# Value and decode products with fp32 operands, 64 weight columns at a time, in place of rounded parts

## The chip, the cores and the metric

The kernel runs on one core of one Trainium2 chip. The metric is the device time in microseconds. Three runs of the kernel before took 702.85, 704.45 and 705.08 us; their median is 704.45.

## The reference

One layer of a hybrid encoder for 1024 prompt tokens and 32 sample tokens, width 1024. A combined projection of the normalized input gives q, k, v, a gate, and the input and gate of a state-space branch. The attention is "stick-breaking": no softmax, strictly causal, 8 heads of 64.

```
z = einsum('bqhd,bkhd->bhqk', q, k) / sqrt(64)
mask = k_pos[None, :] < q_pos[:, None]
log_rem = where(mask, log_sigmoid(-z), 0.0)
after = cumsum(log_rem, axis=3, reverse=True) - log_rem
w = where(mask, exp(log_sigmoid(z) + after), 0.0)
att = einsum('bhqk,bkhd->bqhd', w, v)
```

The 32 sample tokens attend to a cache of 1024 keys and values and to themselves. Then each branch is normalized, gated and multiplied by the output weights, and the sum with the input is normalized.

## The kernel before

Its tensors are fp32. A product at fp32 accuracy is made of rounded parts: an operand is rounded to the type fp32r (the "high" part, a ScalarE copy), the rest is taken by a subtraction on VectorE (the "low" part), and two or three matmuls of such parts are summed in PSUM.

The stages, in order of time: input, projections and the state-space branch (to about 265 us); then the attention pipeline, into which the remaining projections and the state-space half of the output product are woven (to about 632 us); then the attention half of the output product.

The pipeline (`pipeline`, from L1439) has 32 units: 4 pairs of heads, 2 heads h, and 4 query groups j of 256 tokens. A unit's first part (`s1_unit`, L1179) makes the scores of two query blocks (L1163), with the mask as a bf16 product (L1165), and ScalarE takes two sigmoids of them into `cb` and `beta`; VectorE runs a product scan over `cb` (L1208), and POOL or VectorE multiplies `beta` by it, which gives the weights. Two units later the second part (`s3_unit`, L1252) transposes the weights on TensorE into a PSUM bank of the tag tr, of which there are two (L1307), and `wt_split` (L1243) makes of the bank the tiles wth (ScalarE) and wtl (VectorE). A visit to the value product (L1270) takes two key blocks: for each, the stacked values vS, 128 columns that hold the high part of 64 channels and the low part, times wth and times wtl, 256 columns. The halves of the sum are added when it is taken out (`end`, L1277). Visits wait in a queue `pvq` that holds at most LAG = 2, or fewer when one of three buffers of wth and wtl is wanted again.

Two decode units stand among the 32 (`DEC`). `decode_s1` (L1332) loads the cache keys into `kc_raw` (two buffers), splits each tile into wth and wtl, and multiplies with a block-diagonal q of 128 columns (BDh, BDl), three matmuls of 512 columns a tile (L1359). `decode_s3` (L1373) transposes the weights, splits them and the cache values, and sums three matmuls of 256 columns a block (L1384).

What stands between these instructions on TensorE is set by `weave` (L1521): each step of the pipeline yields a cost in ns, times a ratio and with corrections by step number (`MORE`), and so much of the projections (L440) or of the output product (L1626) is emitted behind it. Engines run their queues in order; the order is fixed when the program is built.

The form of the changed products is in the kernel before already: L913 multiplies fp32 operands with 64 weight columns, and its four products of a group go to the two halves of the PSUM partitions in turn:

```
for r in range(2):
    for g2 in range(2):
        nc.tensor.matmul(pb[g2 * 64:g2 * 64 + 64, r * NCH:(r + 1) * NCH],
                         WT[:, r, a, g2 * 64:g2 * 64 + 64], U[:, 2 * a + g2],
                         start=True, stop=True)
```

Of the kernel before, what the change touches and what calls it, by code (L numbers as in the profile page):

```python
# [47 lines left out]
LAG = 2  # L48
MORE = {274: 2000, 268: -500, 119: -1000, 144: -500, 150: 1000, 206: -1500, 322: 500, 329: -1000, 17: 2000, 15: -500, 151: 1500, 131: 500, 125: -1500, 209: 1000, 118: -1000, 114: 1000, 112: 500, 190: -1500, 194: 500}
# [18 lines left out]
def hymba_step(ctx, tc, xT, xn, w_in, ln_g, kcT, vc, w_glu, b_glu, w_out, g_att, g_ssm, final_g,  # L68
# [79 lines left out]
    def open_pair0():  # L148
# [11 lines left out]
        vS[0] = p0.tile([128, 8, 256], F32R, name="vS0")  # L160
        for nm in ("BDh", "BDl"):
            Q[nm] = p0.tile([128, 4, 128], F32R, name=nm)
            nc.gpsimd.memset(Q[nm].bitcast(F32), 0.0)
        Q["KSh"] = p0.tile([128, 4, TS], F32R, name="KSh")
        Q["KSl"] = p0.tile([128, 4, TS], F32R, name="KSl")
# [329 lines left out]
    def split_q(p, st):  # L495
        def evac(i, t0, n, ps):
# [8 lines left out]
            if m < n:  # L505
                for hh in range(2):
                    r = slice(64 * hh, 64 * hh + 64)
                    s = 32 * (2 * (p % 2) + hh)
                    act(Q["BDh"][r, p, s:s + 32], qo[r, m:n])
                    tt(Q["BDl"][r, p, s:s + 32], qo[r, m:n], Q["BDh"][r, p, s:s + 32], OP.subtract)  # L510
        return evac

    def split_k(p, st):
        def evac(i, t0, n, ps):
# [11 lines left out]
            if m < n:  # L526
                act(Q["KSh"][:, p], ko[:, m:n])
                tt(Q["KSl"][:, p], ko[:, m:n], Q["KSh"][:, p], OP.subtract)
        return evac

    def split_v(p, st):
        def evac(i, t0, n, ps):
# [3 lines left out]
            def fin():  # L536
# [8 lines left out]
                stack_v(vS[p % 2][:, b0:b0 + nb], pp[:, :nb * 128].rearrange("p (b c) -> p b c", b=nb))  # L545
# [20 lines left out]

    def stack_v(dst, src):

        for hh in range(2):
            act(dst[:, :, 192 * hh:192 * hh + 64], src[:, :, 64 * hh:64 * hh + 64])  # L570
        for hh in range(2):
            tt(dst[:, :, 64 + 64 * hh:128 + 64 * hh], src[:, :, 64 * hh:64 * hh + 64],
               dst[:, :, 192 * hh:192 * hh + 64], OP.subtract)
# [573 lines left out]
    vS[1] = at.tile([128, 8, 256], F32R, name="vS1")  # L1147
# [89 lines left out]
    def w_tiles():  # L1237
        n_w[0] += 1
        while any(i <= n_w[0] - 3 for i, _, _ in pvq):
            pop_pv()  # L1240
        return (at.tile([128, 512], F32R, name="wth", bufs=3), at.tile([128, 512], F32R, name="wtl", bufs=3))

    def wt_split(pp, c0, n, nk=128):  # L1243
        wh, wl = w_tiles()
        if c0:
            for w in (wh, wl):
                nc.gpsimd.memset(w[:, 0:c0].bitcast(F32), 0.0)
        act(wh[:nk, c0:n], pp[:nk, c0:n])
        tt(wl[:nk, c0:n], pp[:nk, c0:n], wh[:nk, c0:n], OP.subtract)
        return wh, wl  # L1250

    def s3_unit(p, h, j, ba, bb_):  # L1252
# [11 lines left out]
        def pv_mm(blocks, wh, wl):  # L1264
            def f():
                if st["n"] == 0:
                    st["ps"] = p_pv()
                for kb, c0 in blocks:
                    for w in (wh, wl):
# [3 lines left out]
                if st["n"] == 2 * nblk:  # L1273
                    end()
            return f
# [19 lines left out]
        for kp in range(j + 1):  # L1295
# [12 lines left out]
            wh, wl = wt_split(pp, 128 if last else 0, 512)  # L1308
            yield 121 * len(lay)
            yield push_pv([n_w[0]], 4 * 262 / 2.4, pv_mm(blocks, wh, wl))  # L1310
# [8 lines left out]
    def k_load(qd, i):  # L1319
        p = 2 * qd + i % 2  # L1320
        kraw[i] = at.tile([128, 512], F32, name="kc_raw", bufs=2)
        nc.sync.dma_start(kraw[i], kcT[p * 128:(p + 1) * 128, 512 * (i // 2):512 * (i // 2) + 512])

    def v_load(qd, i):
        kraw[i] = at.tile([128, 2, 256], F32, name="kc_raw", bufs=2)
# [6 lines left out]
    def decode_s1(qd, out):  # L1332
# [3 lines left out]
        sp = {}  # L1336

        def split(i):
            sp[i] = w_tiles()
            kr = kraw.pop(i)  # L1340
            act(sp[i][0], kr)
            tt(sp[i][1], kr, sp[i][0], OP.subtract)
            if i < 2:
                k_load(qd, i + 2)
            else:
                v_load(qd, i - 2)

        split(0)
        yield 400.0
        for i in range(4):  # L1350
            p = 2 * qd + i % 2
            if i < 3:
                split(i + 1)
            if i % 2 == 0:
                ps = p_z()
            kh, kl = sp.pop(i)
            bh, bl = Q["BDh"][:, p], Q["BDl"][:, p]
            for n, (a, b) in enumerate(((bh, kh), (bl, kh), (bh, kl))):
                nc.tensor.matmul(ps, a, b, start=(i % 2 == 0 and n == 0), stop=(i % 2 == 1 and n == 2))  # L1359
# [5 lines left out]
        mms = []  # L1365
        for p in (2 * qd, 2 * qd + 1):
            bh, bl, kh, kl = Q["BDh"][:, p], Q["BDl"][:, p], Q["KSh"][:, p], Q["KSl"][:, p]
            mms += [(bh, kh, 32), (bl, kh, 32), (bh, kl, 32)]
        z_tile(mms, 32, (c[:, 1024:1056], be[:, 1024:1056]), maskb[:, 128:160])
        yield 7 * 55.0  # L1370
        s1_fin(c, be, CW - 1)

    def decode_s3(qd, be):  # L1373
        st = {"n": 0}

        def mm(blocks, wh, wl, vh, vl, nk, last=False):

            def f():
                if st["n"] == 0:
                    st["ps"] = p_pv()  # L1380
                for i, b in enumerate(blocks):
                    ws = slice(128 * b, 128 * b + 128)
# [532 lines left out]
```

## Time and profile before

| | |
|---|---|
| median of three runs | 704.45 us (702.85 to 705.08) |
| profiled execution | 703.05 us, span 701.2 |
| TensorE matmul busy | 637.0 us, 91%, 3834 instructions |
| TensorE weight loads | 573.0 us, 82% |
| VectorE busy | 503.0 us, 72%, 751 instructions |
| ScalarE busy | 352.3 us, 50%, 805 instructions |
| GpSimd busy | 240.3 us, 34%, 369 instructions |
| granted TensorE clock, mean | 0.952 |

PE is TensorE's matmuls, PEld its weight loads, DVE VectorE, ACT ScalarE, POOL GpSimd. The duration of a matmul holds the time to fill and empty the array; how often one can start is read from the distance of two starts. Line numbers are those of the kernel; operations that go through a helper bear its line (L95 ScalarE, L98 VectorE and GpSimd). A row of the timeline has start, duration, engine, line, operation, out<-in, shape, count, and in brackets the idle time before it with what ended it. A row of the waits has who waited, for whom, us in total, times, the longest. A row of the windows has the stretch and its length, then busy us and instructions running of PE, PEld, DVE, ACT and POOL (those that have any), the granted clock, the DMA share and GB/s.

### The profile page before, as it was taken

What the parts mean: (1) busy time and instruction counts of PE and PEld (TensorE: products, weight loads), DVE (VectorE), ACT (ScalarE), POOL (GpSimd) and SP (SyncE); (2) the same over time, 40 slices, a digit from 0 to 9 for tenths busy, and PEclk for the clock granted to TensorE, in tenths of its full rate; (3) what the DMA queues carried; (4) which work ended last, traced back from release to release, by engine and by line L of the source; (5) the groups of instructions that cost most, each with busy time, mean ns of one, the idle gap of its engine ahead of it and who ended that gap; (6) DMA issues with size and microseconds to landing.
All of it is one profiled execution on the core that took longest, in us unless ns stands there. A gap on an engine that the chain in (4) does not pass through costs nothing. (4 is left out here: it accounts for less than half of the span.)

```text
span 701.2 us, 10842 instructions
## 1 busy us (share of the span) xinstructions
PE 637.0 (91%) x3834; PEld 573.0 (82%) x3834; DVE 503.0 (72%) x751; ACT 352.3 (50%) x805; POOL 240.3 (34%) x369
## 2 busy tenths in 40 slices
PE   7887799989999998999799999989987798989994
PEld 7887689878999997899788898978886586877872
DVE  6987999895254583787787857776768959775653
ACT  6543232431455553567665675465675645642332
POOL 0510110100123377343444424341326513232885
PEclk9987899999999998999999999999999899999998
DMA  8303514822611162101221012222262584518552
GB/s 301 84 31 78 154 31 119 256 75 97 214 56 37 45 241 109 48 31 57 66 77 55 31 62 92 65 74 69 64 208 75 177 267 129 150 68 273 177 177 97
DMA packets 62645, 79.14 MB, mean 113 GB/s; under 512 B 8864, under 2 KB 47072, under 8 KB 62592
## 3 DMA queue, kind: packets, MB, share of 16 engines
q1 hardware_dynamic: 56112, 66.90, 30.1%
q10 hardware_dynamic: 6480, 11.56, 5.3%
q8 instruction: 30, 0.49, 0.3%
q14 instruction: 23, 0.19, 0.1%
HBM read 51.97 MB, written 26.48 MB: 112 GB/s over the span
## 5 line engine op out<-in xcount | busy, mean ns | idle before, releaser
L440 PE MATMUL pj<-xh,w_hi 128*128 128x256 f32 (+2 forms) x456 | 159.4, 350 | 0.0
L440 PE MATMUL pj<-xl,w_hi 128*128 128x256 f32 (+2 forms) x456 | 149.4, 328 | 0.0
L440 PE MATMUL pj<-xh,w_lo 128*128 128x256 f32 (+2 forms) x456 | 149.0, 327 | 0.0
L1208 DVE TENSOR_TENSOR_SCAN cb<-cb 128x896 f32<-128x896 f32 (+8 forms) x66 | 95.9, 1459 | 6.9 <-ACT cb L95 6.2
L440 PEld LDWEIGHTS pj<-xh,w_hi 128*128 128x128 f32 x456 | 88.8, 195 | 4.3 <-issue 2.4
L440 PEld LDWEIGHTS pj<-xl,w_hi 128*128 128x128 f32 x456 | 88.5, 194 | 1.4
L440 PEld LDWEIGHTS pj<-xh,w_lo 128*128 128x128 f32 x456 | 87.9, 193 | 0.3
L95 ACT ACTIVATE cb<-z 128x512 f32<-128x512 f32 (+4 forms) x102 | 49.8, 489 | 50.0 <-PE z L1165 16.5
L98 DVE TENSOR_TENSOR wtl<-tr,wth 128x512 fp32r<-128x512 f32 (+2 forms) x86 | 53.5, 626 | 27.1 <-ACT wth L95 26.0
L1626 PE MATMUL pj<-xh,S 128*128 128x512 f32 (+3 forms) x212 | 69.8, 409 | 0.5 <-ACT w_raw L95 0.5
L98 POOL TENSOR_TENSOR betaL<-betaL,cb 128x896 f32<-128x896 f32 (+2 forms) x24 | 41.7, 1737 | 71.6 <-DVE cb L1208 41.5
L98 POOL TENSOR_TENSOR w_lo<-w_raw,w_hi 128x512 fp32r<-128x512 f32 x30 | 47.0, 1568 | 36.2 <-ACT w_hi L95 36.0
L98 POOL TENSOR_TENSOR betaS<-betaS,cb 128x128 f32<-128x128 f32 (+3 forms) x32 | 27.8, 872 | 72.6 <-DVE cb L1208 54.1
L95 ACT ACTIVATE wth<-tr 128x512 fp32r<-128x512 f32 (+2 forms) x86 | 47.4, 553 | 10.4 <-PE tr L1307 5.9
L1626 PE MATMUL pj<-xl,S 128*128 128x512 f32 (+3 forms) x112 | 43.7, 393 | 0.9 <-DVE xl L98 0.9
L1270 PE MATMUL pv<-wth,vS 128*128 128x256 f32 x160 | 44.2, 297 | 0.1
L1626 PEld LDWEIGHTS pj<-xh,S 128*128 128x128 f32 (+2 forms) x212 | 37.8, 191 | 7.6 <-ACT w_raw L95 0.8
L1307 PE MATMUL tr<-ident,betaL 128*128 128x128 f32 x208 | 33.4, 278 | 11.3 <-DVE wtl L98 8.0
L1270 PE MATMUL pv<-wtl,vS 128*128 128x256 f32 x160 | 42.2, 286 | 1.5 <-DVE wtl L98 1.5
L98 DVE TENSOR_TENSOR kv_out<-pj,rsx 128x256 f32<-128x256 f32 (+2 forms) x55 | 28.2, 512 | 19.3 <-PE pj L440 16.9
L1307 PEld LDWEIGHTS tr<-ident,betaL 128*128 128x128 f32 x208 | 24.3, 141 | 16.8 <-DVE wtl L98 10.4
L95 ACT ACTIVATE betaL<-z 128x512 f32<-128x512 f32 (+4 forms) x70 | 36.0, 514 | 0.0
(339 smaller groups left out, 1515.5 us busy)
## 6 DMA issues: line engine op xcount, KB each, us to landing
w_raw<-in_w_in ACTq DMA_DIRECT2D x44, 256.0 KB, 2.6
x<-in_xn SPq DMA_DIRECT2D x8, 512.0 KB, 4.8
yp_d<-x SPq DMA_DIRECT2D x8, 512.0 KB, 5.4
x<-yp_d SPq DMA_DIRECT2D x8, 512.0 KB, 4.8
y_out<-x SPq DMA_DIRECT2D x8, 512.0 KB, 2.9
xr<-in_xT SPq DMA_DIRECT2D x7, 528.0 KB, 7.7
wraw<-in_w_out SPq DMA_DIRECT2D x5, 512.0 KB, 5.2
ud<-uj SPq DMA_DIRECT2D x4, 532.0 KB, 5.9
```

The costliest lines, as they stand in the source:

```text
L95: nc.scalar.activation(out, in_, f, **kw)
L98: (eng or nc.vector).tensor_tensor(out, a, b, op)
L440: nc.tensor.matmul(ps[:, :n], a[:, k], b[:, k, t0:t0 + n], start=(k == 0 and f == 0), stop=(k == KT - 1 and f == 2))
L1208: nc.vector.tensor_tensor_scan(cc[:, ::-1], cc[:, ::-1], cc[:, ::-1], 1.0, OP.mult, OP.bypass)
L1270: nc.tensor.matmul(st["ps"][:, 0:256], vs[:, kb, 128 * h:128 * h + 128], w[:, c0:c0 + 256], start=(st["n"] == 0), stop=(st["n"] == 2 * nbl ...
L1307: nc.tensor.transpose(pp[:, c0:c0 + 128], b[:, 128 * kb:128 * kb + 128], ident)
L1626: nc.tensor.matmul(ps[:a.shape[1], :m], a, b_, start=(k == 0 and f == 0), stop=(k == 3 and f == len(mms) - 1))
```

## The change

The rounded parts go. The transposed weights are copied to one fp32 tile `wt` (four buffers, ScalarE), the values to one fp32 tile, and a visit makes one fp32 product for each of its two key blocks, with 64 value columns as weights, even blocks into PSUM partitions 0 to 63 and odd ones into 64 to 127. Decode takes the cache tiles as they come from DMA: one product for each key tile, for one half; two for each value block, one for each half. `kc_raw` has four buffers. Line numbers of the kernel after are 1 to 35 different from those of before.

```diff
-        for nm in ("BDh", "BDl"):
-            Q[nm] = p0.tile([128, 4, 128], F32R, name=nm)
+        Q["BD"] = p0.tile([128, 4, 64], F32, name="BD")
...
-                stack_v(vS[p % 2][:, b0:b0 + nb], pp[:, :nb * 128].rearrange("p (b c) -> p b c", b=nb))
+                act(vS[p % 2][:, b0:b0 + nb], pp[:, :nb * 128].rearrange("p (b c) -> p b c", b=nb))
...
-        while any(i <= n_w[0] - 3 for i, _, _ in pvq):
+        while any(i <= n_w[0] - NWT for i, _, _ in pvq):
...
-        act(wh[:nk, c0:n], pp[:nk, c0:n])
-        tt(wl[:nk, c0:n], pp[:nk, c0:n], wh[:nk, c0:n], OP.subtract)
-        return wh, wl
+        act(w[:nk, c0:n], pp[:nk, c0:n])
+        return w
...
                 for kb, c0 in blocks:
-                    for w in (wh, wl):
-                        nc.tensor.matmul(st["ps"][:, 0:256], vs[:, kb, 128 * h:128 * h + 128], w[:, c0:c0 + 256],
-                                         start=(st["n"] == 0), stop=(st["n"] == 2 * nblk - 1))
-                        st["n"] += 1
+                    r = slice(64 * (kb % 2), 64 * (kb % 2) + 64)
+                    nc.tensor.matmul(st["ps"][r, 0:256], vs[:, kb, 64 * h:64 * h + 64], w[:, c0:c0 + 256],
+                                     start=(st["n"] < 2), stop=(st["n"] >= nblk - 2))
+                    st["n"] += 1
...
-        kraw[i] = at.tile([128, 512], F32, name="kc_raw", bufs=2)
+        kraw[i] = at.tile([128, 512], F32, name="kc_raw", bufs=4)
...
-            for n, (a, b) in enumerate(((bh, kh), (bl, kh), (bh, kl))):
-                nc.tensor.matmul(ps, a, b, start=(i % 2 == 0 and n == 0), stop=(i % 2 == 1 and n == 2))
+            nc.tensor.matmul(ps[64 * (i % 2):64 * (i % 2) + 64], Q["BD"][:, p], kraw.pop(i), start=True, stop=True)
...
-                    for n, (w, v) in enumerate(((wh, vh), (wl, vh), (wh, vl))):
-                        nc.tensor.matmul(st["ps"][:, 0:256], w[0:nk, ws], v[0:nk, 256 * i:256 * i + 256],
-                                         start=(st["n"] == 0), stop=(last and n == 2))
-                        st["n"] += 1
+                    for r in (0, 64):
+                        nc.tensor.matmul(st["ps"][r:r + 64, 0:128], w[0:nk, 128 * b + r:128 * b + r + 64],
+                                         v[0:nk, i, 2 * r:2 * r + 128], start=(st["n"] == 0), stop=last)
+                    st["n"] += 1
```

On TensorE a visit to the value product in the second head of the first pair stands before like this (vS: stacked values, wth and wtl: parts of the weights, pj: a projection's bank, z: scores):

```order
1286 L440 MATMUL pj<-xl,w_hi 128x384
1287 L440 MATMUL pj<-xh,w_lo 128x384
1288 L1270 MATMUL pv<-wth,vS_1713 128x256
1289 L1270 MATMUL pv<-wtl,vS_1713 128x256
1290 L1270 MATMUL pv<-wth,vS_1713 128x256
1291 L1270 MATMUL pv<-wtl,vS_1713 128x256
1292 L440 MATMUL pj<-xh,w_hi 128x384
```

The same visit on TensorE after:

```order
1277 L439 MATMUL pj<-xl,w_hi 128x384
1278 L439 MATMUL pj<-xh,w_lo 128x384
1279 L1257 MATMUL pv<-wt,vS_1713 64x256 x2
1280 L439 MATMUL pj<-xh,w_hi 128x384
1281 L439 MATMUL pj<-xl,w_hi 128x384
```

Its place between the projections is the same; four full-width matmuls have become two half-width ones.

In the first decode unit, TensorE before has three matmuls for a key tile, with the split tiles (wth, wtl) as operands, behind a value product:

```order
2258 L1270 MATMUL pv<-wtl,vS_1713 128x256
2259 L1359 MATMUL z<-wth,BDh 128x512
2260 L1359 MATMUL z<-wth,BDl 128x512
2261 L1359 MATMUL z<-wtl,BDh 128x512
2262 L440 MATMUL pj<-xh,w_hi 128x384
```

After, TensorE has one product for a key tile, with the tile as DMA brought it (kc_raw):

```order
2105 L1257 MATMUL pv<-wt,vS_1713 64x256 x2
2106 L439 MATMUL pj<-xh,w_hi 128x384
2107 L439 MATMUL pj<-xl,w_hi 128x384
2108 L439 MATMUL pj<-xh,w_lo 128x384
2109 L1327 MATMUL z<-kc_raw,BD 64x512
2110 L439 MATMUL pj<-xh,w_hi 128x384
```

A step of projection has come between the last value product and the first key product, and each key product stands by itself between full-width matmuls.

## Rows read from the trace of the kernel before

**Rows 1.** Windows, the attention pipeline.
```profile
285.00:632.00 347.00, 316.77 (x1950) 283.54 (x1950) 264.99 (x363) 210.21 (x492) 128.09 (x160) 0.97 0.29 93
```
**Rows 2.** Waits of PE, 285 to 632 us.
```profile
PE tr L1307 <- DVE wtl L98: 8.0, 9, 2.5
PE z L1359 <- DVE wtl L98: 4.0, 2, 2.4
PE pv L1384 <- DVE wtl L98: 3.3, 3, 2.3
PE z L1163 <- ACT kA L95: 3.0, 2, 2.5
...
PE pv L1270 <- DVE wtl L98: 1.5, 2, 1.1
```
**Rows 3.** Groups of PE: count, busy us, mean ns, idle before.
```profile
L1270 PE MATMUL pv<-wth,vS 128*128 128x256 f32 x160 | 44.2, 297 | 0.1
```
**Rows 4.** Timeline of PE, two visits to the value product.
```profile
299.02 0.28 PE L1270 MATMUL pv<-wth,vS 128*128 128x256 f32 x1
...
299.48 0.34 PE L440 MATMUL pj<-xh,w_hi 128*128 128x384 f32 x1
...
331.57 0.29 PE L1270 MATMUL pv<-wth,vS 128*128 128x256 f32 x1
...
332.05 0.27 PE L1307 MATMUL tr<-ident,betaL 128*128 128x128 f32 x1
```
**Rows 5.** Timeline of PE around a group of L913.
```profile
142.77 0.35 PE L440 MATMUL pj<-xh,w_lo 128*128 128x416 f32 x1
143.06 0.67 PE L913 MATMUL tr<-U,WT 128*64 128x133 f32 x8
...
143.96 0.35 PE L440 MATMUL pj<-xl,w_hi 128*128 128x416 f32 x1
144.15 0.35 PE L440 MATMUL pj<-xh,w_lo 128*128 128x416 f32 x1
```
**Rows 6.** Windows inside that group, L913 alone (PE and PEld).
```profile
143.05:143.10 0.05, 0.04 (x2) 0.04 (x2) 1.00 1.04 410
...
143.32:143.36 0.04, 0.04 (x6) 0.04 (x4) 1.00 0.65 256
...
143.43:143.47 0.04, 0.04 (x6) 0.04 (x2) 1.00 1.18 461
```
**Rows 7.** Timeline of PE, second decode unit, first key tile.
```profile
556.16 0.39 PE L1359 MATMUL z<-wth,BDh 128*128 128x512 f32 x1
556.39 0.40 PE L1359 MATMUL z<-wth,BDl 128*128 128x512 f32 x1
559.17 0.70 PE L1359 MATMUL z<-wtl,BDh 128*128 128x512 f32 x1 [2.39 <-DVE wtl L98]
```
**Rows 8.** Groups of DVE, 285 to 632 us.
```profile
L98 DVE TENSOR_TENSOR wtl<-tr,wth 128x512 fp32r<-128x512 f32 (+2 forms) x84 | 52.2, 625 | 26.8 <-ACT wth L95 25.7 <-POOL betaS L98 0.5
```
**Rows 9.** Timeline of DVE, the same place as rows 7.
```profile
557.02 1.52 DVE L1208 TENSOR_TENSOR_SCAN cb<-cb 128x512 f32<-128x512 f32 x1
558.46 0.66 DVE L98 TENSOR_TENSOR wtl<-kc_raw,wth 128x512 fp32r<-128x512 f32 x1
```
**Rows 10.** Timeline of ACT ahead of a wait for transposes.
```profile
618.06 0.42 ACT L95 ACTIVATE kv_out<-attT 128x256 f32<-128x256 f32 x1 [1.94 <-DVE attT L98]
618.38 1.07 ACT L95 ACTIVATE wth<-tr 128x512 fp32r<-128x512 f32 x2
```
**Rows 11.** Timeline of PE, that wait.
```profile
620.33 0.44 PE L1307 MATMUL tr<-ident,betaL 128*128 128x128 f32 x2 [1.88 <-DVE wtl L98]
```
**Rows 12.** Windows at the lower clock.
```profile
436.40:439.80 3.40, 3.40 (x18) 3.40 (x17) 2.88 (x5) 3.08 (x8) 1.37 (x2) 0.50 0.19 66
...
559.30:562.70 3.40, 3.40 (x9) 2.62 (x10) 3.15 (x7) 0.63 (x1) 0.77 (x1) 0.50 0.39 131
...
620.70:624.10 3.40, 3.40 (x15) 3.11 (x14) 2.22 (x4) 0.92 (x3) 1.02 (x3) 0.51 0.27 82
```

More of the change, by code (lines that the diff above doesn't have):

```diff
@@ L159, in open_pair0 @@
         nc.gpsimd.memset(kL[0][0:64].bitcast(F32), 0.0)
-        vS[0] = p0.tile([128, 8, 256], F32R, name="vS0")
-        for nm in ("BDh", "BDl"):
-            Q[nm] = p0.tile([128, 4, 128], F32R, name=nm)
-            nc.gpsimd.memset(Q[nm].bitcast(F32), 0.0)
-        Q["KSh"] = p0.tile([128, 4, TS], F32R, name="KSh")
-        Q["KSl"] = p0.tile([128, 4, TS], F32R, name="KSl")
+        vS[0] = p0.tile([128, 8, 128], F32, name="vS0")
+        Q["BD"] = p0.tile([128, 4, 64], F32, name="BD")
+        nc.gpsimd.memset(Q["BD"], 0.0)
+        Q["KS"] = p0.tile([128, 4, TS], F32, name="KS")
         Q["p"] = p0
@@ L526, in evac @@
             if m < n:
-                act(Q["KSh"][:, p], ko[:, m:n])
-                tt(Q["KSl"][:, p], ko[:, m:n], Q["KSh"][:, p], OP.subtract)
+                act(Q["KS"][:, p], ko[:, m:n])
         return evac
@@ L565, in ga_evac @@
         return evac
[L567 to L573, printed above, removed]
     def drain(g):
@@ L1146, in hymba_step @@
     nc.gpsimd.memset(kL[1][0:64].bitcast(F32), 0.0)
-    vS[1] = at.tile([128, 8, 256], F32R, name="vS1")
+    vS[1] = at.tile([128, 8, 128], F32, name="vS1")
     NC_ = 2
@@ L1235, in push_pv, with w_tile, wt_copy @@
         return c
-    def w_tiles():
+    def w_tile():
         n_w[0] += 1
-        while any(i <= n_w[0] - 3 for i, _, _ in pvq):
+        while any(i <= n_w[0] - NWT for i, _, _ in pvq):
             pop_pv()
-        return (at.tile([128, 512], F32R, name="wth", bufs=3), at.tile([128, 512], F32R, name="wtl", bufs=3))
-    def wt_split(pp, c0, n, nk=128):
-        wh, wl = w_tiles()
+        return at.tile([128, 512], F32, name="wt", bufs=NWT)
+    def wt_copy(pp, c0, n, nk=128):
+        w = w_tile()
         if c0:
-            for w in (wh, wl):
-                nc.gpsimd.memset(w[:, 0:c0].bitcast(F32), 0.0)
-        act(wh[:nk, c0:n], pp[:nk, c0:n])
-        tt(wl[:nk, c0:n], pp[:nk, c0:n], wh[:nk, c0:n], OP.subtract)
-        return wh, wl
+            nc.gpsimd.memset(w[:, 0:c0], 0.0)
+        act(w[:nk, c0:n], pp[:nk, c0:n])
+        return w
     def s3_unit(p, h, j, ba, bb_):
@@ L1262, in s3_unit, with pv_mm @@
             nc.sync.dma_start(tg, tga_d[:, p, 256 * j:256 * j + 256])
-        def pv_mm(blocks, wh, wl):
+        def pv_mm(blocks, w):
             def f():
@@ L1307, in s3_unit @@
                 nc.tensor.transpose(pp[:, c0:c0 + 128], b[:, 128 * kb:128 * kb + 128], ident)
-            wh, wl = wt_split(pp, 128 if last else 0, 512)
+            w = wt_copy(pp, 128 if last else 0, 512)
             yield 121 * len(lay)
-            yield push_pv([n_w[0]], 4 * 262 / 2.4, pv_mm(blocks, wh, wl))
+            yield push_pv([n_w[0]], 4 * 262 / 2.4, pv_mm(blocks, w))
     def chain(*gs):
@@ L1320, in k_load @@
         p = 2 * qd + i % 2
-        kraw[i] = at.tile([128, 512], F32, name="kc_raw", bufs=2)
+        kraw[i] = at.tile([128, 512], F32, name="kc_raw", bufs=4)
         nc.sync.dma_start(kraw[i], kcT[p * 128:(p + 1) * 128, 512 * (i // 2):512 * (i // 2) + 512])
     def v_load(qd, i):
-        kraw[i] = at.tile([128, 2, 256], F32, name="kc_raw", bufs=2)
+        kraw[i] = at.tile([128, 2, 256], F32, name="kc_raw", bufs=4)
         if i == 4:
@@ L1335, in decode_s1 @@
         out.append(be)
[L1336 to L1342, printed above, removed]
+        for i in range(4):
+            p = 2 * qd + i % 2
+            if i % 2 == 0:
+                ps = p_z()
+            nc.tensor.matmul(ps[64 * (i % 2):64 * (i % 2) + 64], Q["BD"][:, p], kraw.pop(i), start=True, stop=True)
             if i < 2:
@@ L1364, in decode_s1 @@
             yield DY
[L1365 to L1370, printed above, removed]
+        ps = p_z()
+        for i in range(2):
+            r = slice(64 * i, 64 * i + 64)
+            nc.tensor.matmul(ps[r, :TS], Q["BD"][:, 2 * qd + i], Q["KS"][:, 2 * qd + i], start=True, stop=False)
+            nc.tensor.matmul(ps[r, :TS], identb[:, r], maskb[:, 128:160], start=False, stop=True)
+        act(c[:, 1024:1056], ps[:, :TS], AF.Sigmoid, scale=-SC)
+        act(be[:, 1024:1056], ps[:, :TS], AF.Sigmoid, scale=SC)
+        yield 600.0
         s1_fin(c, be, CW - 1)
@@ L1374, in decode_s3, with mm @@
         st = {"n": 0}
-        def mm(blocks, wh, wl, vh, vl, nk, last=False):
+        def mm(blocks, w, v, nk, last=False):
             def f():
```

37 lines of the change are left out of this document (8 added, 29 removed).

## The prediction, made before the result was known

> **What bounds the kernel now.** I read the windows first, because the change touches one stage only: everything from the first attention unit to the end of the pipeline, 285 to 632 us. There TensorE is busy 316.8 of 347 us, VectorE 265, ScalarE 210, at a granted clock of 0.97 of full speed, which is a mix of the two levels 2.4 and 1.2 GHz [rows 1]. So TensorE is the bound, with 30.2 us of idle time; what the change adds to TensorE's own work is paid in full, and what it can give back is some of those 30.2 us and of the clock. The second view is who TensorE waited for in that stretch: 8.0 + 4.0 + 3.3 + 1.5 = 16.8 us are waits for the rounded rest wtl that VectorE makes, the first before transposes (L1307: their PSUM bank is free only when wtl has been subtracted from it), the next two in the decode units, the last in the value products [rows 2]. The other 13.4 us are waits for other things, such as kA. The third view is the order of time around single places, for prices.
>
> **What the change adds on TensorE.** The product with the values now takes two matmuls of 256 columns per key block (wth and wtl), 160 blocks in all [rows 3], two blocks to a visit, so 80 visits. Four starts and the next instruction's start lie 0.46 us apart in one visit and 0.48 in another [rows 4]; I take 0.47.
>
> After, a visit is two fp32 products with 64 weight columns, one in each half of the PSUM partitions. Before has that very form, with 133 columns: L913. One group of four products stands between L440 matmuls: from the last L440 start ahead of it, 142.77, to the second L440 start behind it, 143.96, are 1.19 us; two of them are L440's own spacing of 0.19 [rows 5], so the group takes 0.81. It has eight instructions for four products, thus two passes each. The stretches show that they begin by twos: two run at 143.05, six by 143.36, and in 143.43 to 143.47 still six although the first two, begun at 143.06, have by then ended, so all eight have begun [rows 6]. The last two start thus at about 143.45, 0.39 after the first, and the two before them at about 143.34: a step is 0.11 us. Four steps are 0.45, and 0.81 - 0.45 = 0.36 us is what going in and out of the half-width form costs: about 0.1 before it, 0.05 at the first step, 0.2 before L440 runs again at its pace. At 256 columns a step is 0.11 x 256/133 = 0.215, so a visit takes 2 x 0.215 + 0.36 = 0.79, that is 0.32 more than now, and 80 visits make +25.6 us.
>
> The Trainium skill, TensorEngine Tiling (Array Packing), section Theoretical Speedup, gives up to 2x for a weight side of 64 or less; by that alone a visit would take 0.43 and 80 visits would save 3 us. The same page, section Key Properties, says that a change of tiling mode drains the engine, and gives no price; the trace's 0.36 us around L913 is that price, and it speaks against the change.
>
> Decode, same reckoning. Value products: 54 matmuls of 256 columns at 0.12 are 6.3 us; after, eight visits of four steps at 128 columns, 4 x 0.11 + 0.36 = 0.80, and two of two steps, 0.58: 7.5, so +1.2. Scores: 24 matmuls of 512 columns at 0.23 [rows 7] are 5.5; after, each of eight products stands alone in its half, with other work between, two passes of 0.43 and 0.36: 9.8, so +4.3. The 32-column score products are a handful on both sides; I cost the difference at nothing, since they are less than a microsecond in a unit that waits far longer for its sigmoids. Sum: 25.6 + 1.2 + 4.3 = +31 us. Lower bound: where a visit follows a wait, going in costs nothing (0.26 instead of 0.36), so some 23. Upper bound: if the two halves did not overlap at all, a visit takes 4 x 0.215 + 0.36 = 1.22, and the 80 alone cost +60. The nearest row, L913, is the same form, so I stay near its price: +30.
>
> **What it gives back.** VectorE loses the subtractions: 52.2 us for the 84 of the weights [rows 8], and with the decode and value ones some 70 of its 265. ScalarE loses only the decode copies, since it copies the transposed weights as before.
> (a) Decode. The clearest wait: a score matmul ready at 556.6 starts at 559.17 after 2.39 us [rows 7], because its wtl stands in VectorE's queue behind a 1.52 us scan and runs at 558.46 [rows 9]. After, the raw cache tile is the operand and comes by DMA into one of four buffers instead of two, issued some microseconds ahead, and no engine stands between. Of 4.0 + 3.3 + 1.5 = 8.8 us I take back 8. If the cover is gone (a DMA that lands late), TensorE waits for it directly.
> (b) Transposes. Not all 8.0 us go, since the ScalarE copy that then frees the bank can itself be late: in the 1.88 us wait that ends at 620.33 [rows 11] the two copies ran from 618.38 on, held up in ScalarE's queue by a square that waits for VectorE [rows 10]. The bank would have been free some 1.4 us earlier. I take 5 of 8.
> (c) The other 13.4 us are chains in which VectorE's queue is one link; with a quarter less in that queue I take a third, 4. Zero is the lower bound, 8 the upper.
> (d) A matmul that restarts after a wait runs long (0.70 us against 0.40 in [rows 7]); with some 20 waits fewer at about 0.1, 2.
> (e) Clock. Seven stretches of 3.4 us in the stage run at the lower level, 0.50 [rows 12], and each stands behind one of the longer waits of (a) and (b): 559.30 right behind the wait that ended at 559.17, 620.70 behind 620.33, four of the seven in decode units. Each costs half its length, 1.7; I take five of seven, 8.5. None would be the other end; new ones can come only if new waits do.
> Sum: 8 + 5 + 4 + 2 + 8.5 = 27.5.
>
> POOL clears one tile instead of two per diagonal (32 times), which hides behind TensorE either way. The value tile's evacuation is one copy instead of two and two subtractions; it shortens a chain off the path, nothing. A new wait is not added to any queue: the value product waits for the ScalarE copy, which wtl had waited for as well.
>
> **Sum.** The profiled execution took 703.05 us (span 701.2 and 1.85 around it), 1.4 under the median of the runs, 704.45, and inside their range. 703.05 + 30 - 27.5 = 705.5; with the half microsecond by which such a run lies low against the median, 706. It is a small difference of two large terms, and the range must carry both errors.
>
> **Rivals.**
> A, faster: the waits on VectorE go altogether. 16.8 us of wtl, 8 of the others, 2 of restarts and all 12 of the clock are 39, against 30 to 31: 695 to 697. For it: in decode and transposes VectorE is named in all the longest waits, and VectorE falls from 265 to some 195 busy. Against: the copy of [rows 10] is late for another reason, and kA waits [rows 2] are a latency that an emptier queue only shortens. It decides from a return of about 32 on. Chance 0.28.
> B, slower by more: the waits go over to ScalarE. The bank, the weight tile and the score banks then all hang on its in-order queue, where a copy stands behind squares and sigmoids that wait for VectorE's chain; if (b), (c) and half of the clock stay, the return is 8 + 2 + 2 + 5 = 17 and the time 716. For it [rows 10], against it that ScalarE is busy only 210 of 347. Chance 0.14.
> C, slower still: the passes of the two halves do not pair. If the engine took the passes strictly in program order, the first product's second pass would hold up the second product, and a visit would have three steps instead of two: 80 x 0.215 = 17 more, 723. Against it: in [rows 6] two begin at once from the first step, which a strict order would not do. The Trainium skill, TensorE: Matmul & The Clock Gate, Part 3 (The mechanism), says that matmuls keep program order in start and end; by that rule C holds, and L913's rows so far speak against it. Chance 0.08.
> The forecast, 700 to 712 with 706 as its middle, has 0.50.
>
> **How the numbers follow.** A measurement of this kernel tells a difference from about 0.3% on, 2.1 us: faster is below 702.3, slower above 706.6. Rival A gives faster 0.28; the forecast's own lower edge adds 0.07, its middle 0.20 to no change, its upper part 0.23 to slower; B and C add 0.22. So 0.35, 0.20, 0.45. The range takes in most of A and B: lowest costs with a high return (30 - 38) give 695, highest cost with a low return (33 - 17) 719; C and the far end of A stay outside. The likeliest case alone is 700 to 712.
>
> **What would show it.** Right: 160 products of the values as 320 half-width instructions that begin by twos, a visit near 0.79 us; TensorE's busy time from the first attention unit to the pipeline's end up by about 30 minus what the clock gives; no wait of TensorE for a subtraction in decode; VectorE some 70 us less busy there; three or fewer stretches at the low clock. Wrong: a visit of 1.0 us or more (C), or of 0.5 (no price for going in and out), waits for ScalarE's copy in the place of those for wtl (B), idle time under 5 us (A), or TensorE waiting for kc_raw from DMA.

## The result, and the profile after

The changed kernel takes 696.87 us (696.58 to 698.65, 4 runs), the kernel before, in the same comparison, 703.95 (702.85 to 705.08, 4 runs). The ratio is 0.9905 [0.9881, 0.9929]: the change makes the kernel 1% faster. The time lies in the range that was forecast, on the other side of no change from the 706 us named, and 9 us below it.

The stretch from 285 to 632 us of the kernel after, to be laid beside [rows 1]:

```profile
285.00:632.00 347.00, 336.48 (x2003) 249.90 (x2002) 205.49 (x243) 201.15 (x469) 123.47 (x138) 0.99 0.31 98
```

TensorE is busy 336.5 us instead of 316.8, so 10.5 us are idle (3.2 of them the beginning of the wait for S shown below), where there were 30.2. VectorE has 59 us less work in this stretch (65 over the same work, cut as below; the forecast had some 70), ScalarE 9. The clock stands at 0.99 of full speed instead of 0.97.

From the list of TensorE's waits in that stretch, beside [rows 2] (for whom, us in total, times, the longest; between the two rows stand 2.0 us for VectorE's x and 1.2 for its kv_out):

```profile
PE tr L1294 <- ACT wt L96: 2.4, 2, 1.7
...
PE pv L1257 <- POOL wt L1234: 0.8, 1, 0.8
```

No wait for wtl is left, and the wait for ScalarE's copy that took over (rival B) is 2.4 us, not 8. The second row is a wait for POOL's clearing of a quarter of the weight tile, which by the prediction "hides behind TensorE either way"; here it doesn't.

A visit to the value product, between projections with 256 and with 384 columns, first before and then after (timeline of TensorE):

```profile
315.09 0.28 PE L440 MATMUL pj<-xh,w_lo 128*128 128x256 f32 x1
315.21 0.28 PE L1270 MATMUL pv<-wth,vS 128*128 128x256 f32 x1
...
315.69 0.34 PE L440 MATMUL pj<-xh,w_hi 128*128 128x384 f32 x1
315.86 0.34 PE L440 MATMUL pj<-xl,w_hi 128*128 128x384 f32 x1
```

```profile
317.62 0.28 PE L439 MATMUL pj<-xh,w_lo 128*128 128x256 f32 x1
317.83 0.65 PE L1257 MATMUL pv<-wt,vS 128*64 128x256 f32 x4
318.42 0.44 PE L439 MATMUL pj<-xh,w_hi 128*128 128x384 f32 x1
318.70 0.33 PE L439 MATMUL pj<-xl,w_hi 128*128 128x384 f32 x1
```

From the start of the matmul ahead to the second start behind, 0.77 us have become 1.08. That is 0.31 more; the forecast had 0.32. A visit comes 0.21 instead of 0.12 us behind its predecessor, and the projection behind it needs 0.28 instead of 0.17 until the next starts. The four instructions begin by twos, as windows with this line alone show (PE and PEld):

```profile
317.84:317.88 0.04, 0.04 (x2) 0.04 (x2) 1.00 0.00 0
...
318.05:318.09 0.04, 0.04 (x2) 0.00 (x0) 1.00 0.00 0
318.12:318.16 0.04, 0.04 (x4) 0.00 (x0) 1.00 0.00 0
```

Two run from the first window on and four in the window from 318.12, so the visit has two steps, not three: rival C is out.

For what follows, the stage is cut at the same four matmuls in every kernel: the 721st L440, the 113th L1163, the last projection but one, and the 241st matmul of the output product. In the first third the order of TensorE's work is the same in before and after, the decode units stand in the other two. Windows of before, then of after:

```profile
264.03:443.10 179.07, 166.35 (x1088) 155.28 (x1087) 130.38 (x184) 109.89 (x260) 79.11 (x93) 0.97 0.19 61
443.10:532.52 89.42, 82.53 (x517) 75.29 (x517) 64.87 (x90) 55.45 (x131) 30.75 (x36) 0.96 0.31 97
532.52:645.25 112.73, 98.62 (x511) 79.48 (x510) 86.32 (x118) 57.72 (x134) 37.15 (x66) 0.94 0.52 162
```

```profile
265.36:444.22 178.86, 174.16 (x1087) 141.35 (x1086) 101.28 (x120) 109.55 (x253) 73.91 (x77) 0.98 0.19 60
444.22:528.84 84.62, 83.74 (x520) 63.33 (x520) 48.10 (x56) 50.76 (x122) 30.64 (x30) 1.00 0.34 104
528.84:641.22 112.38, 104.28 (x516) 67.43 (x515) 66.80 (x83) 52.05 (x123) 35.10 (x56) 0.94 0.53 171
```

The stage is 381.2 us long before and 375.9 after, 5.4 less, nearly all of it in the second third. Its idle time (length less PE) went from 33.7 to 13.7, and the time at the lower clock level from 30.6 us in eight stretches (the seven that the prediction counts and one of 6.8 us at 269) to 20.4 in three of 6.8. The prediction's sign "three or fewer stretches" is thus met in number, but by length only a third of that time went.

One wait is new, and the longest: at the end of the woven part the output product of the attention half waits for its operand S. Timeline of TensorE and ScalarE, and the window behind it:

```profile
628.49 0.28 PE L1591 MATMUL pj<-xl,S 128*64 128x256 f32 x1
632.26 0.79 PE L1591 MATMUL z<-xh,S 128*128 128x512 f32 x1 [3.49 <-ACT S L96]
```

```profile
631.58 0.63 ACT L96 ACTIVATE S<-O 128x512 fp32r<-128x512 f32 x1 [2.48 <-DMA O<-att_d]
```

```profile
631.80:635.20 3.40, 2.94 (x6) 2.10 (x7) 2.24 (x4) 1.35 (x3) 1.01 (x3) 0.50 0.89 276
```

ScalarE's copy waits for the attention result to come back by DMA, nothing else stands ahead of that product in TensorE's queue, and the clock is at half behind it.

### The profile page after: what moved, and what is told of

Its sections match the earlier page's. It is cut to its first block, busy times and chain, and to the rows that moved or that the text cites. A ratio compares the mean times of both kernels' runs of the same rounds, so it can differ in the third digit from the quotient of the medians.

```text
span 694.9 us, 10575 instructions
## 1 busy us (share of the span) xinstructions
PE 652.9 (94%) x3842; PEld 536.3 (77%) x3842; DVE 437.6 (63%) x611; ACT 341.8 (49%) x775; POOL 232.3 (33%) x336
## 5 line engine op out<-in xcount | busy, mean ns | idle before, releaser
L439 PE MATMUL pj<-xh,w_hi 128*128 128x256 f32 (+2 forms) x456 | 163.2, 358 | 0.0
L439 PE MATMUL pj<-xl,w_hi 128*128 128x256 f32 (+2 forms) x456 | 147.8, 324 | 0.0
L439 PE MATMUL pj<-xh,w_lo 128*128 128x256 f32 (+2 forms) x456 | 147.5, 324 | 0.0
L1196 DVE TENSOR_TENSOR_SCAN cb<-cb 128x896 f32<-128x896 f32 (+8 forms) x66 | 98.5, 1499 | 19.0 <-ACT cb L96 18.8
L1591 PE MATMUL pj<-xh,S 128*128 128x512 f32 (+3 forms) x212 | 71.2, 414 | 2.2 <-DVE x L1595 2.0
L96 ACT ACTIVATE wt<-tr 128x512 f32<-128x512 f32 (+2 forms) x86 | 47.2, 551 | 20.0 <-PE tr L1294 14.4
L1257 PE MATMUL pv<-wt,vS 128*64 128x256 f32 x320 | 52.4, 407 | 0.8 <-POOL wt L1234 0.8
L99 DVE TENSOR_TENSOR attT<-pv,attT 64x256 f32<-64x256 f32 x32 | 13.4, 420 | 34.7 <-ACT attT L96 34.5
L96 ACT ACTIVATE w_hi<-w_raw 128x512 fp32r<-128x512 f32 x44 | 27.6, 630 | 15.1 <-DMA w_raw<-in_w_in 13.1
L1257 PEld LDWEIGHTS pv<-wt,vS 128*64 128x64 f32 x320 | 16.0, 135 | 20.2 <-issue 14.6
```

The lines of the kernel that those rows point to most:

```text
L96: nc.scalar.activation(out, in_, f, **kw)
L99: (eng or nc.vector).tensor_tensor(out, a, b, op)
L439: nc.tensor.matmul(ps[:, :n], a[:, k], b[:, k, t0:t0 + n], start=(k == 0 and f == 0), stop=(k == KT - 1 and f == 2))
L1196: nc.vector.tensor_tensor_scan(cc[:, ::-1], cc[:, ::-1], cc[:, ::-1], 1.0, OP.mult, OP.bypass)
L1257: nc.tensor.matmul(st["ps"][r, 0:256], vs[:, kb, 64 * h:64 * h + 64], w[:, c0:c0 + 256], start=(st["n"] < 2), stop=(st["n"] >= nblk - 2))
L1591: nc.tensor.matmul(ps[:a.shape[1], :m], a, b_, start=(k == 0 and f == 0), stop=(k == 3 and f == len(mms) - 1))
```

## The experiments

Below, the price is what the change adds to TensorE's own work, and the return is what it takes away of waits and of time at the low clock. A price by spacing is read from the distance between the starts of the instructions around a product. All times are medians; the kernel before, run beside them, had 702.84, 703.08, 703.22, 702.99 and 701.85 us in the five comparisons.

**The return without the price.** The subtractions for weights and cache tiles go; the split of the prompt's values and the number and form of the matmuls stay:

```
-        tt(wl[:nk, c0:n], pp[:nk, c0:n], wh[:nk, c0:n], OP.subtract)
...
+        w = at.tile([128, 512], F32R, name="wth", bufs=3)
+        return w, w
```

> The kernel before without its subtractions for weights, cache keys and cache values: the high part stands in the low part's place, so the low parts are left out of these products; TensorE's instructions are the same in number and form. It shows what the waits on VectorE are worth with no price on TensorE. By the prediction's sum (27.5 us back) 675 to 678; if the return was under-estimated, as the result says (some 35), 667 to 671. Over 685: the gain of the change has another source than the subtractions.

Measured: 676.48 us, ratio 0.9639 [0.9588, 0.9691]. The same three thirds:

```profile
267.95:437.87 169.92, 162.90 (x1088) 152.59 (x1087) 109.92 (x140) 109.19 (x260) 76.83 (x77) 0.99 0.19 63
437.87:518.54 80.67, 78.08 (x517) 72.28 (x516) 50.13 (x64) 54.99 (x131) 30.75 (x29) 1.00 0.35 109
518.54:620.88 102.34, 93.70 (x511) 75.84 (x510) 69.24 (x84) 57.54 (x134) 37.22 (x57) 0.98 0.57 178
```

The stage shrinks by 28.3 us: 15.5 of idle time and 12.8 of TensorE's busy time, with 6.8 us at the low clock instead of 30.6; half of such time is lost, so this is 11.9 of the 12.8. The forecast's 27.5 was right, and nearly so in its parts: 17 of idle time, 10.5 of restarts and clock. (By the times of the runs the return is 25 to 26.) So the mistake is not in the return, and 676.5 + 30 is still 706: it must lie in the price, or in how it is paid.

**The price without the return.** The kernel after, with VectorE's subtraction of the weights still made into a tile that nobody reads:

```
         act(w[:nk, c0:n], pp[:nk, c0:n])
+        d = at.tile([128, 512], F32, name="wtl", bufs=2)
+        tt(d[:nk, c0:n], pp[:nk, c0:n], w[:nk, c0:n], OP.subtract)
```

> The kernel after, with VectorE's subtraction of the transposed weights put back (its result is used by nothing, but it reads the PSUM bank and holds it). TensorE's work is that of after. Theory 1 (VectorE's queue and its hold on the bank made the waits): waits before transposes come back, 8 us and some clock with them, 707 to 714. Rival (the gain comes from more buffers, or from the fp32 operands standing ready sooner, not from VectorE): within 2 us of the kernel after, 695 to 699.

Measured: 704.84, ratio 1.0047 [1.0014, 1.0079], 8 to 10 us above the kernel after, just under what the theory gave. TensorE waits again for transposes held up by that subtraction:

```profile
PE tr L1296 <- DVE wtl L99: 5.0, 7, 2.3
```

**The price alone.** The kernel without the return's work (676.5) with the value products of the changed kernel; the split of the prompt's values goes with it (14 subtractions fewer, 7 us of VectorE's time in the first third), and the order of the work is that of before:

```
-                    for w in (wh, wl):
-                        nc.tensor.matmul(st["ps"][:, 0:256], vs[:, kb, 128 * h:128 * h + 128], w[:, c0:c0 + 256],
...
+                    r = slice(64 * (kb % 2), 64 * (kb % 2) + 64)
+                    nc.tensor.matmul(st["ps"][r, 0:256], vs[:, kb, 64 * h:64 * h + 64], w[:, c0:c0 + 256],
```

> The kernel without the rounding subtractions and low parts (676.5 us) with one thing added: the value products of the changed kernel, fp32 with 64 weight columns in two halves; the order of the work and the decode units are those of the kernel before, with the high part in the place of the low one in decode. The visits' price is 80 times about 0.30 us, 24 us, read from the traces (0.85 to 1.16 us from one neighbour's start to the second behind). Theory 1 (paid in full): 700 to 701. Theory 2 (a fifth to two fifths falls into waits of TensorE, as 15 of 37 us did with the doubled passes): 691 to 696, with the idle time of the stage below the 18 us of the kernel without the price.

Measured: 688.11, ratio 0.9785 [0.9728, 0.9843]. Of 24 us by spacing only 10 to 12 are paid, so the time is below what either theory gave. The thirds:

```profile
267.46:445.76 178.30, 173.17 (x1087) 140.35 (x1086) 102.90 (x126) 109.34 (x253) 74.79 (x77) 0.99 0.18 60
445.76:528.99 83.23, 81.94 (x517) 67.10 (x517) 48.53 (x58) 54.86 (x129) 30.75 (x29) 1.00 0.34 106
528.99:633.72 104.73, 99.24 (x511) 69.73 (x510) 68.41 (x84) 57.52 (x134) 37.07 (x57) 0.97 0.56 174
```

Against the kernel without the price the stage is 13.3 us longer. TensorE is busy 19.7 more and idle 6.3 less (18.2 to 11.9). So 6.3 us of the price came out of idle time, and some 4 of the 24 by spacing don't even show as busy time: a visit that follows a wait grows by less (the one in the rows below is busy for 0.73 us in the old form and 0.65 in the new). Whether that is all of these 4 us is not shown. The thirds hold 40, 18 and 22 visits, by 0.30 us 12.0, 5.4 and 6.6; they grow by 8.4, 2.6 and 2.4. How it goes at one place: the 70th visit waits for POOL to clear its weight tile, here without the price and then with it (timeline of TensorE).

```profile
566.38 0.60 PE L1415 MATMUL tr<-ident,betaL 128*128 128x128 f32 x4
...
567.52 0.64 PE L1269 MATMUL pv<-wth,vS 128*128 128x256 f32 x4
...
571.17 0.73 PE L1269 MATMUL pv<-wth,vS 128*128 128x256 f32 x4 [2.31 <-POOL wth L1247]
```

```profile
577.85 0.60 PE L1429 MATMUL tr<-ident,betaL 128*128 128x128 f32 x4
...
579.08 0.65 PE L1283 MATMUL pv<-wt,vS 128*64 128x256 f32 x4
...
582.07 0.65 PE L1283 MATMUL pv<-wt,vS 128*64 128x256 f32 x4 [1.46 <-POOL wt L1260]
```

The visit ahead takes 0.3 us longer, and the next one waits 0.85 less. POOL's clearing, behind a 4.0 us product in POOL's queue, ends when the other engines let it, and a dearer visit ahead only moves TensorE's arrival toward that time: 0.3 of the 0.85. The other 0.55 is there before: from the start of the transposes to the end of the wait are 4.79 us without the price and 4.22 with it, so TensorE came to them later against POOL; that the dearer visits before this place made it late is inferred. All waits of this kind, without the price and then with it:

```profile
PE pv L1269 <- POOL wth L1247: 6.1, 4, 2.3
```

```profile
PE pv L1283 <- POOL wt L1260: 3.4, 4, 1.5
```

**Another added cost.** To see whether this belongs to the new form or to any added work, the kernel without the price issues each value product twice as often in the old form:

```
-                    for w in (wh, wl):
+                    for w in (wh, wl, wl, wl):
```

> The kernel without the rounding subtractions and low parts (676.5 us), in which each value product is issued four times instead of twice on TensorE, with the same operands, the same order and no other work; the sums are those of four passes. A pass of 256 columns takes 0.116 us in the trace, two further ones for each of 160 blocks are 37 us of TensorE's own time. Theory 1 (what is added to TensorE's work is paid in full, as the prediction had it): 676.5 + 37 = 713 to 714. Theory 2 (part of the added time is filled into waits that TensorE has anyway, since the other engines get on meanwhile; some 5 us of the 18 that the stage still idles): 706 to 709, with idle time in the stage down from 18 us to 13 or less.

Measured: 698.66, ratio 0.9931 [0.9909, 0.9954]: 21 to 22 of 37 us paid, again less than either theory gave. A visit has grown by 0.46 at the usual places (850 to 1308 ns between projections of 416 columns, medians of 13), as reckoned. The stage's thirds:

```profile
266.75:451.68 184.93, 180.69 (x1248) 171.94 (x1246) 106.28 (x141) 109.95 (x260) 74.85 (x77) 0.98 0.18 59
451.68:537.21 85.53, 85.08 (x588) 80.48 (x588) 50.41 (x64) 56.03 (x134) 30.47 (x30) 1.00 0.33 102
537.21:643.13 105.92, 101.06 (x600) 84.84 (x598) 67.74 (x83) 56.70 (x132) 37.20 (x56) 1.00 0.55 173
```

TensorE is busy 32.2 us more, its idle time falls from 18.2 to 9.5, and the last third, 22 visits with 10 us more to do, is only 3.6 longer. So it is not the form. The stage is 23.4 us longer for 37 added here and 13.3 for 24 with the visits alone: of work added to an engine that is the bound, but idles for 18 us, about two fifths were filled in. (The times of the runs say up to a half, but hold the time outside the stage too, 323.5 us in the profile without the price, 322.2 and 321.5 in these two.) The clock is not the reason: 6.8 us at the low level in the stage without the price, 10.2 with the visits, 6.8 here.

**Each half of the change alone.** The decode products alone in the new form, and the value products alone (with decode as before):

> Only the decode units take fp32 operands as they come (three key and value buffers instead of four, for space); the prompt's value product keeps its rounded parts. Theory 1: +5 us of TensorE work, 8.8 us of waits and four slow-clock stretches (6.8) gone, so 693 to 697. Theory 2: more than that, 688 to 692, since then decode must carry the whole gain against a loss outside. If it is 700 or more, decode's waits only move.

> Only the prompt's value product takes the fp32 half-width form (fp32 copies of weights and values); the decode units keep their rounded parts. Theory 1 (the return of waits was under-estimated everywhere, price of a visit as predicted, 0.79 us against 0.47): +25 us of TensorE work and about as much back, so 702 to 706. Theory 2 (the sizes of the prediction hold outside decode; all the unforeseen gain is decode's): +25 against some 15 back, 712 to 716. TensorE's waits before transposes fall below 3 us under both.

Measured: decode alone 695.06, ratio 0.9911 [0.9879, 0.9942]; values alone 698.48, ratio 0.9932 [0.9895, 0.9968]. Decode alone is where theory 1 put it; the values alone were forecast as a loss by the prediction's terms, and they gain, below both theories. The halves gain 6.3 and 4.8 us (ratios times 703), together 11, and the whole change 6.7. What they share is the clock: 30.6 us at the low level in the stage before, 10.2 with decode alone, 10.2 with the values alone, and with both 20.4, so each half by itself gets 10.2 us back and the whole change 5.1. In idle time they don't get in each other's way: 33.7 us before, 33.8 with decode alone, 18.1 with the values alone, 13.7 with both. By these profiles decode's gain is thus the clock's: the waits of its products for wtl go, but others, the wait for S among them, come in their place. With the values alone, the decode waits for wtl where [rows 2] had 3.3 and 4.0 are

```profile
PE pv L1398 <- DVE wtl L98: 2.5, 4, 1.0
PE z L1373 <- DVE wtl L98: 2.3, 2, 2.0
```

and those for ScalarE's copy are 2.3, where there were 1.2: of 8.5 us of decode waits 7.1 are left, so VectorE's shorter queue takes back little of them.

**Buffers.** After has one more weight tile and two more cache tiles; here as many as before (`NWT = 3`, `kc_raw` with `bufs=2`):

> The changed kernel with three tiles for the transposed weights instead of four, and two buffers for the raw cache tiles instead of four, as many as before the change. Theory 1 (the gain comes from the subtractions that went, not from deeper buffers): 696 to 699. Rival (part of the idle time that went, some 5 us, went because the tiles are freed later without harm): 701 to 705, with waits of TensorE or ScalarE for a buffer.

Measured: 695.07, ratio 0.987 [0.9854, 0.9887], a little under theory 1. The buffers are no part of the gain.

**Fewer trips into the half-width form.** Visits are issued in twos (shown), and in threes (there the condition is `len(pvq) > LAG + two`, with six weight tiles):

```
+        if len(pvq) > LAG:
+            while len(pvq) > LAG - two:
+                c += pop_pv()
```

> The changed kernel with the value products of two visits issued one behind the other where the order allows it: 43 stretches in the half-width form instead of 79. Theory 1 (0.36 us of a visit is going in and out of the half-width form; the one place where two visits already stand together shows 0.38 us for the second instead of 0.78): 36 stretches fewer by 0.38 us are 14 us, so 682 to 686, if the deeper queue of value products makes no new waits. Rival (the 0.36 us belongs to each product, as slower first passes): 696 to 698.

> The changed kernel with up to three visits one behind the other and six tiles for the transposed weights: 32 stretches in the half-width form instead of 79. Theory 1: 47 stretches fewer by 0.38 us are 18 us, so 678 to 682; less is gained if weights that are used later, and a longer stretch without other work, hold up the transposes, then some 684 to 690. Rival (the price belongs to each product): 696 to 698.

Measured: 711.52, ratio 1.0114 [1.0071, 1.0157], and 706.54, ratio 1.0038 [1.001, 1.0065]: both expectations missed. The price is where it was thought to be, as the place between 256 and 384 columns shows for twos:

```profile
362.49 0.28 PE L439 MATMUL pj<-xh,w_lo 128*128 128x256 f32 x1
362.70 1.08 PE L1258 MATMUL pv<-wt,vS 128*64 128x256 f32 x8
...
364.00 0.34 PE L439 MATMUL pj<-xl,w_hi 128*128 128x384 f32 x1
```

1.51 us for two visits where one takes 1.08: the second costs 0.43, and 0.35 is saved. But the second visit now comes before its weight tile is ready:

```profile
389.32 0.65 PE L1258 MATMUL pv<-wt,vS 128*64 128x256 f32 x4
393.15 0.65 PE L1258 MATMUL pv<-wt,vS 128*64 128x256 f32 x4 [3.18 <-POOL wt L1235]
```

While this visit waits, TensorE does nothing, since it stands at the head of the queue. The stage's idle time is 36.0 us with twos (389.7 long, 353.7 busy) and 30.6 with threes, against 13.7 in the kernel after. What the trips gave came back as waits, and more.

**The value product on the whole array.** 128 weight columns, no halves:

```
-                    nc.tensor.matmul(st["ps"][r, 0:256], vs[:, kb, 64 * h:64 * h + 64], w[:, c0:c0 + 256],
+                    nc.tensor.matmul(st["ps"][:, 0:256], vs[:, kb, 0:128], w[:, c0:c0 + 256],
```

> The changed kernel with each value product on the whole array: 128 weight columns (both heads of the pair) instead of 64, all key blocks of a unit summed in one PSUM range, so no half-width form in the prompt part; two fp32 passes for each of 160 blocks, none beside another. The other head's sum is added in at the end of a unit, so the outputs are not those of the reference there. The form has 2 x 2 steps of 0.216 us in a visit instead of 2. Theory 1 (0.36 us of a visit of 0.78 is going in and out of the half-width form): a visit takes 0.86 us or a little more, the kernel 697 + 78 x 0.08 = 700 to 705. Rival (the 0.36 us belongs to fp32 operands): 1.2 us in a visit, 697 + 33 = 720 to 730 less what falls into waits.

Measured: 703.6, ratio 1.0016 [0.9997, 1.0034]. The same place in the timeline:

```profile
319.48 0.28 PE L439 MATMUL pj<-xh,w_lo 128*128 128x256 f32 x1
319.60 1.03 PE L1257 MATMUL pv<-wt,vS 128*128 128x256 f32 x4
...
320.64 0.34 PE L439 MATMUL pj<-xl,w_hi 128*128 128x384 f32 x1
```

The visit follows at the usual 0.12 us, and the whole takes 1.16 instead of 1.08. Less the neighbours' own 0.12 and 0.17 it is 0.86: four steps of 0.216, and no price at either end. So 0.35 of a half-width visit is going in and out. Here 78 visits by 0.08 are 6.2 us, and the time is 6.7 (medians) to 7.8 (ratios) more, inside theory 1. That looks like a price paid in full, but the profiles don't show it so: the stage is 4.8 us longer (380.7), with 2.6 more of idle time and 3.4 us at the low clock instead of 20.4, so more than the visits' price has changed.

**The planner's number.** It reckons 437 ns for a visit:

```
-            yield push_pv([n_w[0]], 4 * 262 / 2.4, pv_mm(blocks, w))
+            yield push_pv([n_w[0]], 780.0, pv_mm(blocks, w))
```

> The changed kernel with one number of the planner altered: it reckons 780 ns for a visit of the value products, as measured, instead of 437, so that work for the waits is laid out later and less of it is needed. Theory 1 (after the change TensorE is busy for nearly all of the stage, 13.7 us idle, and what order it has matters little): 694 to 699. Rival (the planner, told too low a price, puts other work where it comes too late, some 5 us): 690 to 693. If the new order makes waits as the order in twos did, over 700.

Measured: 705.79, ratio 1.0046 [1.0027, 1.0065], a miss for both theories; what came is the case named last. The truer number gives an order that is 9 to 10 us slower. The wait for S has grown from 3.5 to 7.5 us, and the last third from 112.4 to 123.4. The order of the work alone can cost as much as the whole change gains, much of it at a single place.

**The decode scores on the whole array.** With the buffers of before, and 128 weight columns, half of them zero:

```
-            nc.tensor.matmul(ps[64 * (i % 2):64 * (i % 2) + 64], Q["BD"][:, p], kraw.pop(i), start=True, stop=True)
+            nc.tensor.matmul(ps, Q["BD"][:, p], kraw.pop(i), start=(i % 2 == 0), stop=(i % 2 == 1))
```

> The changed kernel with the buffers of before (695.1 us), in which the decode scores run on the whole array: 128 weight columns, of which the 64 that belong to the other product of the tile are zero, both products summed in one PSUM tile. The order of the work is the same. Each of these products stands alone in its half with nothing beside it, so the half-width form halves nothing: 0.48 and 0.52 us for its two passes and 0.2 for its neighbours, against two passes of 0.43. Theory 1 (0.35 us is the price of going in and out of the half-width form, and the decode units are bound by TensorE there): eight times 0.35 less, 2.8 us, so 692 to 693, faster than the kernels before and after the change. Rival (in the decode units what TensorE saves turns into waiting for the sigmoids): 695 to 696.

Measured: 694.39 (691.7 to 695.85), ratio 0.9895 [0.9869, 0.9921]. It beats the kernel before by 1%; against 695.07 with these buffers and the half-width scores it can't be told apart, so the time decides between theory 1 and the rival no more than the profiles do, in which the second and last third are 2.2 us shorter.

## Why the prediction was wrong

**The step that failed** is the first one: "what the change adds to TensorE's own work is paid in full". The stage's sum in the terms of the forecast: return 28.3 measured, 27.5 forecast. Value visits: 23.5 us by their spacing (78 by about 0.30), 25.6 forecast, but 13.3 paid in the stage. From there to the kernel after, which has decode in the new form as well, the stage is 9.6 longer (366.3 to 375.9); forecast were 5.5. Together -28.3 + 13.3 + 9.6 = -5.4, where the forecast, taken at 30, had +2.5. The first term is 12 us too high, the decode term 4 too low.

The mistake behind it: the same 30.2 us of idle time were used on one side only. The return took 17 of them, and the 13 that stayed were treated as if TensorE were busy then. Those waits end at times that other engines set, and work added ahead of them comes out of the wait. What is shown is that about two fifths of added work is filled in, in two forms that have little else in common, and at one wait how.

The decode term stays open in part. By spacing, the eight scores grow from 0.70 to 1.21 us each, 4.1 in all as forecast (4.3), while the value visits take some 7.5 us in both forms (6.3 and 7.5 forecast). What no row of before shows is the wait for S: 3.5 us, with 6.8 us at the low clock behind it, half of which is lost. The wait stands in each of the nine profiles with the new decode products (3.1 to 3.5 us in six, with 3.4 us at the low clock behind it in the other five of these; 2.0 to 7.5 in twos, threes and with the planner's number), and in none of the five with the old ones (before, values alone, no subtraction, price alone, doubled passes). These 6.9 us and the 4.1 of the scores are more than the 9.6 paid; as this step also drops ScalarE's copies and changes the buffers and the order of the work, how the 9.6 divide is not shown. Why the order with the new products leaves TensorE without work at that point was not tried; that an order alone can move the kernel by 10 us, the planner's number shows.

**Smaller slips in the sum.** The prediction gives 23 us as a lower bound of the price, but its range begins with "lowest costs" of 30; with 23 and a return of 27.5 it would have had 698.5. The profiled execution lies 1.4 us under the median, of which half a microsecond was added back. And three of the seven stretches at the low clock (436, 470, 497) stand behind waits of at most 1.1 us, not behind one of the longer ones.

**What held.** The price of a visit at the usual places (0.31 against 0.32), got from L913 in another stage at another width; its 0.36 for going in and out, 0.35 here. The size of the return, and that the clock is a large part of it. The pairing of the halves. That kc_raw from DMA makes no wait in the changed kernel: none is in the list (1.1 us in the last experiment, 0.3 in two others).

**The rivals.** A gave the time, 695 to 697, but not by its reason: it kept the price whole and let all waits go, a return of 39; the return was 28. B is out by the 2.4 us of waits for ScalarE's copy, C by the pairs. The Trainium skill, TensorE: Matmul & The Clock Gate, Part 3 (The mechanism), says that matmuls keep program order in start and end; C took this rule for single passes, and so it is not borne out: two begin within the same 0.04 us window, and a visit has two steps. For whole products the rows don't speak against it. The Trainium skill, TensorEngine Tiling (Array Packing), section Key Properties, says that a change of mode drains the engine; the visit's rows agree in that it starts 0.09 us later than usual and the projection behind it needs 0.11 more, but don't show a drain itself, as the ends of matmuls in a profile are modelled. By these runs the price of going in and out is 0.35 us.

**The size of what can be read from one profile.** In the first third the kernel with decode alone changed runs the instructions of before and takes 176.6 us instead of 179.1, with no time at the low clock there instead of 10.2 us. A term below some 2.5 us is thus not told apart by single profiles.

## What to carry to other kernels

Don't add a price to the bound engine's time and a return from its waits as if they were independent: work added to an engine that idles for other engines' latencies is partly filled in, here about two fifths of it in two cases. How much depends on where the work and the waits stand; no run here gives a rule for it. Measure the return without the price first (here one run); then it is known how much idle time is left for the price to fall into. And before work is grouped to save a fixed cost, look at when its operands are ready: at the head of an in-order queue an early instruction stops everything behind it.

## What the runs showed of the hardware that was not expected

fp32 products with 64 weight columns in two halves gain hardly anything over the whole array at 256 columns: 0.08 us a visit, since 0.43 of stepping are saved and 0.35 lost at the two ends. Where a product has no partner in the other half, the half-width form is a loss: a decode score of 512 columns on the whole array lets the work behind it follow sooner, though too little to be seen in the kernel's time (694.39 against 695.07). First after (half-width), then the whole array:

```profile
553.94 0.40 PE L1591 MATMUL pj<-xl,S 128*128 128x512 f32 x1
554.26 1.07 PE L1327 MATMUL z<-kc_raw,BD 128*64 128x512 f32 x2
555.27 0.73 PE L1591 MATMUL pj<-xh,S 128*128 128x512 f32 x2
```

```profile
553.04 0.40 PE L1591 MATMUL pj<-xl,S 128*128 128x512 f32 x1
553.27 1.02 PE L1327 MATMUL z<-kc_raw,BD 128*128 128x512 f32 x2
553.73 1.03 PE L1591 MATMUL pj<-xh,S 128*128 128x512 f32 x2
```

The row behind the scores begins 1.33 us after the row ahead in the first and 0.69 in the second; 0.34 of that is kept, since the pair of matmuls in it then takes 1.03 instead of 0.73.
